# A list scheduler's durations set from a trace, and its priorities changed over 41 trial schedules, in a two-block transformer forward pass

## Chip, core and metric

One core of a Trainium2 chip runs the whole program in one launch. The metric is the device time of one execution in microseconds (us); each figure for a kernel is the median of several executions. TensorE does matmuls (PE in the rows; PEld is its weight load), VectorE is DVE, ScalarE is ACT, GpSimd is POOL, and SyncE (SP) issues most DMAs. Every engine takes its instructions strictly in the order in which they stand in its own stream.

## What is computed

Two transformer layers on 256 tokens of width 1024, batch 1, all in float32. The reference, cut to its frame:

```python
h = rms_norm(x, norm_attn_pre)
parts = split_cols(h @ w_in, IN_SPLITS)
o_a, o_b, o_c, o_d = nsa(...), dilated(...), forgetting(...), mla(...)   # four attentions
merged = sum(sigmoid(h @ w_merge_gate[i]) * (o_i @ w_i) for i in 4 branches)
x = x + rms_norm(merged @ w_o)
x = x + rms_norm(conv_gated_ffn(rms_norm(x)))          # 1024 -> 2 x 2816 -> 1024
# second layer
x = x + mix(retention(...), differential_attention(...)) @ w_out
x = x + cross_attention(rms_norm(x), rms_norm(mem)) @ xo
x = x + (silu(h @ w_gate) * (h @ w_up)) @ w_down       # h = rms_norm(x)
```

The weights, some 150 MB, are read once.

## The kernel before

**Tiling.** Tokens stand as two tiles of 128 (tt = 0, 1). A large matrix product is made of float32r (fp32r) matmuls in three terms: each weight panel of 512 KB (a tile of class `raw`, 128 x 1024) comes in by a DMA on SP, ScalarE casts it to its high part (`hi`), VectorE subtracts to get the low part (`lo = raw - hi`), and `mm3` adds hi x hi, hi x lo and lo x hi in one PSUM bank. These are the rows `bank<-hi,x`, `bank<-lo,x` (weights moving) and `bank<-x,hi`, `bank<-x,lo` (weights stationary). A panel of 1024 columns feeds 12 matmuls of 512 columns. There are 3 `raw`, 8 `hi` and 8 `lo` buffers, so a DMA waits until ScalarE and VectorE have done with a `raw` buffer, and a cast waits until TensorE has done with a `hi` buffer. Activations are transposed on TensorE against `ident` (rows `bank<-ident,k`), and attention works in plain float32 (rows `bank<-k,k`).

**Attention.** `attend` treats two heads: `scores` (four matmuls that stay together, 128x256 and 128x128 twice), then on VectorE a fused add of the bias with a row minimum (in the trace CUSTOM_DVE_ANT_0 and the read of its accumulator), exponentials on ScalarE, a reciprocal and four scalings on VectorE, two times three transposes of the probabilities on TensorE, two copies out of PSUM (one VectorE, one ScalarE), and `values` (four matmuls 64x256 and 64x128). Branch a (nsa) calls it four times.

**The order.** The program is not emitted as it is written. Class `Plan` records every operation with what it reads and writes (6336 operations: 4160 PE, 1084 DVE, 740 ACT, 52 POOL, 300 SP). `Plan.issue` then runs a model of the five engines in time: an operation becomes ready when its predecessors have ended, plus `NEAR` (100 ns) on the same engine or `FAR` (300 ns) on another; an engine that is free takes the ready one with the lowest `prio` that finds its buffers; and the operations are emitted in the order of their modelled starts. `prio` is the number in the program, less 150 for what isn't bulk weight work, less 300 for what is marked urgent; the first DMAs have -4000. `_Op.cost` gives the modelled duration. Buffers are assigned in the same pass. So durations and priorities set the order on each engine, and nothing else does. The helper that emits every operation is the lambda in `add`, so every row of the trace carries its line, L100.

**Places.** The prediction goes to four places: the start (`mats1`: `x` in halves, `gcol`, the panels of `wi0`); branch a's four calls of `attend`, which stand beside the weights of merge gate 1 (`gate(1, "c")`); the first step of the first FFN (`make_ffn`: `natural`, whose evacuation `ev` copies PSUM to `nat`, and `dnstep`, whose panels come from `in_fdn`); and the remaining stretches in which TensorE idles.

Of the kernel before, what the change touches and what calls it, by code (L numbers as in the profile page):

```python
# [19 lines left out]
class Plan:  # L20
# [138 lines left out]
    def issue(self):  # L159
        ops = self.ops  # L160
        succ = [[] for _ in ops]
        left = [len(o.preds) for o in ops]
        ready = [0.0] * len(ops)
        for o in ops:
            for p in o.preds:
                succ[p.n].append(o)
# [3 lines left out]
        order = {}  # L170
        for o in ops:
            o.own = [nm for nm in o.tiles if nm in self.cls]
            for nm in o.own:
                if self.users[nm][0] is o:
                    order.setdefault(self.cls[nm], []).append(nm)
        ptr = {c: 0 for c in order}
        placed = [False] * len(ops)
# [13 lines left out]
        start = [0.0] * len(ops)  # L191
        while done < len(ops):
# [5 lines left out]
            while pend and pend[0][0] <= t:  # L198
                _, n = heapq.heappop(pend)
                heapq.heappush(heaps[ops[n].eng], (ops[n].prio, n))  # L200
            while rel and rel[0][0] <= t:
                u, c, i = heapq.heappop(rel)
                heapq.heappush(free[c], (u, i))
            for e, hp in heaps.items():
# [24 lines left out]
                if e in ("DVE", "ACT") and not o.urgent:  # L229
                    soon = t + self.PATIENCE * o.cost  # L230
                    if any(r <= soon and ops[m].eng == e and ops[m].urgent for r, m in pend):
                        heapq.heappush(hp, (o.prio, n))
                        continue
                for nm in o.own:
# [4 lines left out]
                    self.real[nm] = self.slots[c][place[nm]]  # L239
                    while ptr[c] < len(order[c]) and order[c][ptr[c]] in place:  # L240
                        ptr[c] += 1
                placed[n] = True
                start[n] = t
                if o.dma:
# [3 lines left out]
                    end = dma_free + 900.0  # L248
# [4 lines left out]
                for s in succ[n]:  # L253
# [3 lines left out]
                    ready[s.n] = max(ready[s.n], end + lat)  # L257
# [4 lines left out]
                for nm in o.tiles:  # L262
                    users[nm] -= 1
                    o_end = max(self.last.get(nm, 0.0), end)
                    self.last[nm] = o_end
                    if not users[nm] and nm in self.cls:
                        heapq.heappush(rel, (o_end + self.FAR, self.cls[nm], place[nm]))
                        heapq.heappush(events, o_end + self.FAR)
        self.length = max(tfree.values())
# [3 lines left out]

    reserve = {"k4": 1, "x8": 2, "k2": 3, "x2": 2, "k1": 2, "sm": 4, "PS": 2}

    @property
    def last(self):
        return self.__dict__.setdefault("_last", {})


class _Op:
    def __init__(self, plan, n, eng, go, name, outs, ins, k):
# [8 lines left out]
        elif eng == "PE":  # L291
            n_ = size if name == "matmul" else 128
            passes = 1 if name == "transpose" or ins[0].dtype == F32R else 4
            least = 107.0
            self.cost = max(least, n_ * passes / 2.4)
        elif eng == "ACT":
            extra = sum(isinstance(k.get(x), bass.AP) for x in ("scale", "accum_out"))
            self.cost = 105.0 + 0.8125 * size + 93.0 * extra
        elif eng == "DVE":
# [3 lines left out]
            self.cost = 65.0 + size * (0.52 if two else 1.042) + (45.0 if name == "scalar_tensor_tensor" else 0.0)  # L303
# [4 lines left out]
    def go(self):  # L308
        for part in self.parts:
            part()  # L310
# [1323 lines left out]
```

## Time and profile before

| | us |
|---|---|
| median of 3 runs | 883.85 (882.42 to 883.87) |
| the profiled execution, its own time | 883.68 |
| its span, first to last instruction | 881.9 |
| TensorE busy in the span | 860.0 (98%) |
| TensorE weight load busy | 717.4 (81%) |
| VectorE busy | 639.2 (72%) |
| ScalarE busy | 492.2 (56%) |
| DMA | 156.08 MB, mean 177 GB/s |

The page gives shares of the whole span; a table by stretches of time shows where an engine idles, the list of waits who ended the idle time, and the timeline one engine's instructions in order. Matmuls overlap each other in the rows, since the end of one is modelled: the time that one costs is read from the distance of the starts of two rows, and a busy TensorE can still be slower than it could be.

### The profile page before, as it was taken

To read this page: it belongs to the slowest core of one execution; us is meant where nothing else is said; L and a number is where in the kernel's file an instruction comes from. 1 tells how busy PE (TensorE), PEld (TensorE's weight loads), DVE (VectorE), ACT (ScalarE), POOL (GpSimd) and SP (SyncE) were. 2 spreads that over 40 slices of the span, in tenths; PEclk is the share of its full clock that TensorE was granted. 3 is DMA by queue.
4 is the path that set the end of the run, shared out by engine and by line. 5 is a ranking of instruction groups with operands and counts; after the bars stand their busy time and mean duration, and the time that the engine had idled before them with its cause. 6 is when DMAs were issued, how large, how long until landed. Compare 5 with 4: busy or idle time off the path is not lost.

```text
span 881.9 us, 12156 instructions
## 1 busy us (share of the span) xinstructions
PE 860.0 (98%) x4436; PEld 717.4 (81%) x4436; DVE 639.2 (72%) x1148; ACT 492.2 (56%) x845; POOL 46.3 (5%) x58
## 2 busy tenths in 40 slices
PE   6999998999999999999999999999999999999998
PEld 5789876788887888888877887788888888888886
DVE  6885558867567998887978687967855777666662
ACT  5775454745455676666754457655644565455441
POOL 2100000000001000000010022211100000000000
PEclk9999999999999999999999999999999999999999
DMA  7556743565457577665636654554633577666541
GB/s 244 184 202 196 228 139 96 184 202 192 146 156 245 161 218 216 200 208 171 211 100 212 191 165 147 166 168 156 201 122 96 160 225 229 194 175 198 185 138 49
DMA packets 45185, 156.08 MB, mean 177 GB/s; under 512 B 5262, under 2 KB 6840, under 8 KB 44996
## 3 DMA queue, kind: packets, MB, share of 16 engines
q1 hardware_dynamic: 44228, 153.10, 55.7%
q0 software_dynamic: 896, 2.19, 1.0%
q8 instruction: 35, 0.57, 0.2%
q14 instruction: 26, 0.21, 0.1%
HBM read 154.21 MB, written 1.06 MB: 176 GB/s over the span
## 4 chain that ended last, share of the span: by engine, by line
PE 83%; DVE 7%; DMA 3%; issue 3%; ACT 2%; POOL 1%; SPq 0%; DVEq 0%; POOLq 0%; ACTq 0%
PE bank L100 83%; DVE k L100 4%; DVE lo L100 2%; ACT k L100 2%; DVE x L100 1%; POOL sm L100 1%; DMA raw<-in_fdn 1%; DVE sm L100 1%; DMA raw<-in_wi 1%; DMA sm<-in_ind 1%; DMA sm<-in_dgain 1%; DMA sm<-in_xgain 0%; ACT x L100 0%; ACT hi L100 0%; SPq L100 0%
## 5 line engine op out<-in xcount | busy, mean ns | idle before, releaser
L100 PE MATMUL bank<-hi,x 128*128 128x512 f32 (+3 forms) x1556 | 497.6, 393 | 1.8 <-ACT x L100 1.7
L100 DVE TENSOR_TENSOR lo<-raw,hi 128x1024 fp32r<-128x1024 f32 (+2 forms) x279 | 335.1, 1208 | 102.3 <-ACT hi L100 99.7
L100 ACT CAST hi<-raw 128x1024 fp32r<-128x1024 f32 (+2 forms) x279 | 288.8, 1040 | 139.1 <-PE bank L100 64.3
L100 PEld LDWEIGHTS bank<-hi,x 128*128 128x128 f32 (+1 forms) x1556 | 290.5, 188 | 58.6 <-ACT x L100 2.3
L100 PE MATMUL bank<-lo,x 128*128 128x512 f32 (+3 forms) x786 | 306.5, 391 | 0.4 <-DVE lo L100 0.4
L100 PE MATMUL bank<-x,hi 128*128 128x512 f32 x656 | 228.7, 398 | 0.0
L100 PE MATMUL bank<-x,lo 128*128 128x256 f32 x656 | 171.0, 281 | 0.0
L100 PEld LDWEIGHTS bank<-lo,x 128*128 128x128 f32 (+1 forms) x786 | 147.3, 187 | 27.7 <-DVE lo L100 1.2
L100 PEld LDWEIGHTS bank<-x,hi 128*128 128x128 f32 x656 | 119.3, 188 | 22.8
L100 PEld LDWEIGHTS bank<-x,lo 128*128 128x128 f32 x656 | 124.0, 189 | 7.5
L100 ACT COPY k<-bank 128x256 f32<-128x256 f32 (+5 forms) x116 | 46.0, 399 | 91.1 <-PE bank L100 90.8
L100 PE MATMUL bank<-ident,k 128*128 128x128 f32 (+2 forms) x362 | 59.9, 283 | 12.2 <-DVE k L100 9.2
L100 PEld LDWEIGHTS bank<-ident,k 128*128 128x128 f32 (+2 forms) x362 | 44.5, 142 | 27.5 <-DVE k L100 14.7
L100 POOL TENSOR_TENSOR sm<-sm,nhalf 128x1 f32<-128x1 f32 (+3 forms) x36 | 36.8, 1024 | 511.5 <-DVE sm L100 501.6
L100 DVE TENSOR_TENSOR x<-bank,x 128x512 fp32r<-128x512 f32 (+4 forms) x62 | 36.7, 609 | 28.6 <-PE bank L100 21.2
L100 PE MATMUL bank<-k,k 64*128 64x256 f32 (+12 forms) x364 | 51.2, 332 | 2.7 <-DVE k L100 1.7
L100 PEld LDWEIGHTS bank<-k,k 64*128 64x128 f32 (+4 forms) x364 | 39.9, 180 | 14.0 <-issue 4.7
L100 DVE TENSOR_TENSOR k<-k,bank 128x256 f32<-128x256 f32 (+1 forms) x78 | 32.5, 418 | 23.9 <-ACT k L100 23.4
L100 ACT ACTIVATE k<-bank 128x512 f32<-128x512 f32 (+4 forms) x41 | 19.4, 480 | 44.7 <-PE bank L100 43.1
L100 ACT CAST x<-bank 128x512 fp32r<-128x512 f32 (+2 forms) x49 | 24.5, 515 | 20.7 <-PE bank L100 20.1
L100 DVE SCALAR_TENSOR_TENSOR k<-k,convw,k 128x255 f32<-128x255 f32 x72 | 34.1, 479 | 1.0 <-ACT k L100 0.4
L100 ACT ACTIVATE k<-bank,sm 128x256 f32<-128x256 f32 (+1 forms) x42 | 22.6, 564 | 16.1 <-PE bank L100 9.5
(97 smaller groups left out, 404.9 us busy)
## 6 DMA issues: line engine op xcount, KB each, us to landing
raw<-in_wi SPq DMA_DIRECT2D x42, 512.0 KB, 4.2
raw<-in_up SPq DMA_DIRECT2D x40, 512.0 KB, 4.2
raw<-in_fup SPq DMA_DIRECT2D x36, 512.0 KB, 4.3
raw<-in_wg SPq DMA_DIRECT2D x32, 512.0 KB, 4.1
raw<-in_fdn SPq DMA_DIRECT2D x22, 512.0 KB, 4.4
raw<-in_dn SPq DMA_DIRECT2D x22, 512.0 KB, 4.5
raw<-in_xkv SPq DMA_DIRECT2D x16, 512.0 KB, 4.5
raw<-in_wo SPq DMA_DIRECT2D x8, 512.0 KB, 4.2
```

Source lines behind the costliest of these rows:

```text
L100: op = _Op(self, n, eng, lambda: getattr(target, name)(*map(self.place, a), **{x: self.place(y) for x, y in k.items()}), name, outs, ins, k)
```

## The change

The set of operations, their shapes and their number on each engine stay as they are: 4250 matmul instructions, 300 DMAs on SP and so on in both programs. What changes is the scheduler. `_Op.cost` has other constants: a float32r matmul n/2.4 + 13.5 ns, a transpose 108, other float32 matmuls at four passes + 3; ScalarE 70 or 120 ns + 0.8125 a column and 75 for each operand of one column; VectorE with a term for scalar operands; POOL's power by its columns, not 700 flat. The modelled end of a DMA is 1700 ns after its data instead of 900. The old body of `issue` becomes `trial(prio)`, which also keeps, for each operation, which predecessor was last (`late`) and who freed the buffer that it lacked (`short`). `hurry` walks over the modelled gaps of TensorE, and for each (the first time all of them, then each with chance 0.4) follows up to 14 steps back from the matmul that waited to what ended last, and takes 20, 60 or 150 off the priority of each operation that stood ready for over 50 ns. `issue` runs `trial` once, then 40 times with hurried priorities, and keeps a schedule only if its modelled length is smaller.

```diff
-    def issue(self):
+    def trial(self, prio):
...
-                heapq.heappush(heaps[ops[n].eng], (ops[n].prio, n))
+                heapq.heappush(heaps[ops[n].eng], (prio[n], n))
...
                         if len(free[c]) < need:
                             ok = False
+                            short[n] = c
...
-                    end = dma_free + 900.0
+                    end = dma_free + 1700.0
...
+        return max(tfree.values()), start, place, (ready, late, short)
+
+    def hurry(self, run, prio, share, pick):
+
+        ops = self.ops
+        _, start, _, (ready, late, short) = run
+        new = list(prio)
+        end = 0.0
+        for o in sorted((o for o in ops if o.eng == "PE"), key=lambda o: start[o.n]):
+            gap = start[o.n] - end
+            if gap > 80.0 and pick.random() < share:
+                n, seen = o.n, 0
+                push = pick.choice((20, 60, 150))
+                while n >= 0 and seen < 14 and start[n] > start[o.n] - 25000.0:
+                    by = short.get(n, -1)
+                    if start[n] - ready[n] > 50.0:
+                        new[n] -= push
+                    n = by if by >= 0 and start[n] - ready[n] > 50.0 and start[by] < start[n] else late[n]
+                    seen += 1
+            end = max(end, start[o.n] + o.cost)
+        return new
+
+    def issue(self):
...
+        pick = random.Random(1)
+        prio = [o.prio for o in ops]
+        best = self.trial(prio)
+        for i in range(self.ROUNDS):
+            other = self.hurry(best, prio, 1.0 if i == 0 else 0.4, pick)
+            try:
+                run = self.trial(other)
+            except RuntimeError:
+                continue
+            if run[0] < best[0]:
+                best, prio = run, other
...
+    ROUNDS = 40
...
-            passes = 1 if name == "transpose" or ins[0].dtype == F32R else 4
-            least = 107.0
-            self.cost = max(least, n_ * passes / 2.4)
+            if name == "transpose":
+                self.cost = 108.0
+            elif ins[0].dtype == F32R:
+                self.cost = n_ / 2.4 + 13.5
+            else:
+                self.cost = max(112.0, n_ * 4 / 2.4 + 3.0)
         elif eng == "ACT":
-            extra = sum(isinstance(k.get(x), bass.AP) for x in ("scale", "accum_out"))
-            self.cost = 105.0 + 0.8125 * size + 93.0 * extra
+            extra = sum(isinstance(k.get(x), bass.AP) for x in ("scale", "bias", "accum_out")) + (name == "mul" and len(ins) > 1)
+            self.cost = (70.0 if ps else 120.0) + 0.8125 * size + 75.0 * extra
...
-            self.cost = 65.0 + size * (0.52 if two else 1.042) + (45.0 if name == "scalar_tensor_tensor" else 0.0)
+            aps = len(ins) > 1 and name in ("tensor_scalar", "scalar_tensor_tensor")
+            self.cost = 65.0 + size * (0.52 if two else 1.042) + (60.0 if aps and two else 20.0 if name == "tensor_tensor_reduce" else 0.0)
+        elif name == "tensor_tensor":
+            self.cost = 420.0 + 155.0 * size
```

**The start, SP's stream.** `x_150` is the first token tile and `x_151` the second, each loaded in two halves of 256 KB; `sm_119` is the gain in columns; `raw_63` to `raw_65` are the first three weight panels. Before:

```order
L100 DMA x_150<-in_x 128x512 x2
L100 DMA sm_119<-in_gcol 128x8
L100 DMA raw_63<-in_wi 128x864
L100 DMA raw_64<-in_wi 128x864
L100 DMA raw_65<-in_wi 128x864
L100 DMA x_151<-in_x 128x512 x2
L100 DMA cst<-in_cst 128x832
```

and now:

```order
L101 DMA x_150<-in_x 128x512 x2
L101 DMA x_151<-in_x 128x512
L101 DMA sm_119<-in_gcol 128x8
L101 DMA raw_63<-in_wi 128x864
L101 DMA raw_64<-in_wi 128x864
L101 DMA raw_65<-in_wi 128x864
L101 DMA x_151<-in_x 128x512
L101 DMA cst<-in_cst 128x832
```

One half of the second token tile (its columns 512 to 1023) now stands ahead of the gain and of the three panels. VectorE's square of that half, which needs it, moves with it: from behind the eight low parts of the first transposes to a place ahead of the two scalings of the first token tile that make its transposes possible.

**Branch a's attention, TensorE's stream,** from the second call's transposes of probabilities to its values (`bank<-ident,k` the transposes, `k,k` with 64 columns the values, `hi` and `lo` weights of merge gate 1). Before, two more groups of transposes follow at once:

```order
L100 MATMUL bank_138<-ident,k_101 128x128 x3
L100 MATMUL bank_136<-ident,k_100 128x128 x3
L100 MATMUL bank_137<-k_96,k_117 64x128
L100 MATMUL bank_137<-k_102,k_117 64x128
L100 MATMUL bank_137<-k_96,k_116 64x256
L100 MATMUL bank_137<-k_102,k_116 64x256
L100 MATMUL bank_135<-ident,k_99 128x128 x3
L100 MATMUL bank_138<-ident,k_94 128x128 x3
L100 MATMUL bank_136<-k_84,k_83 128x256
L100 MATMUL bank_141<-k_84,k_83 128x256
```

and now:

```order
L101 MATMUL bank_137<-ident,k_97 128x128 x3
L101 MATMUL bank_141<-ident,k_99 128x128 x3
L101 MATMUL bank_138<-lo_80,x_90 128x512
L101 MATMUL bank_138<-hi_72,x_90 128x512
L101 MATMUL bank_138<-hi_68,x_91 128x512
L101 MATMUL bank_138<-lo_76,x_91 128x512
L101 MATMUL bank_138<-hi_68,x_91 128x512
L101 MATMUL bank_135<-k_96,k_118 64x128
L101 MATMUL bank_135<-k_101,k_118 64x128
L101 MATMUL bank_135<-k_96,k_116 64x256
L101 MATMUL bank_135<-k_101,k_116 64x256
```

Five weight matmuls stand between the transposes and the values that wait for their copies. Counted over the place: before, from the scores of the first call to the last values there stand 26 weight matmuls, 24 transposes, five groups of scores (one of them branch b's) and three of values. Now the first call's scores stand 129 weight matmuls ahead of the next scores, and from those to the last values there are 39 weight matmuls, 22 transposes, four groups of scores and three of values. VectorE's share of the later stretch falls from 20 bias adds, 16 scalings, 4 low parts and 4 copies to 12, 12, 3 and 4.

**The first FFN step, ScalarE's stream** (`hi<-raw` casts of weight panels, `k<-bank` the copy of `ev`; the cast ahead of the copy is that of the first panel of `in_fdn`). Before:

```order
L100 CAST x_90<-bank_135 128x4x128
L100 CAST x_91<-bank_139 128x4x128
L100 CAST hi_70<-raw_65 128x1024
L100 CAST hi_69<-raw_63 128x1024
L100 CAST hi_72<-raw_64 128x1024
L100 COPY k_98<-bank_136 128x256
L100 CAST hi_68<-raw_65 128x1024
```

and now:

```order
L101 CAST x_90<-bank_138 128x4x128
L101 CAST x_91<-bank_137 128x4x128
L101 CAST hi_67<-raw_65 128x1024
L101 CAST hi_69<-raw_63 128x1024
L101 COPY k_100<-bank_142 128x256
L101 CAST hi_68<-raw_64 128x1024
```

The copy out of PSUM, for which the next transposes wait, has changed places with the cast of the `in_fdn` panel.

## Rows read from the trace of the kernel before

**Rows 1.** The page: the span, each engine's busy time (share of the span) and number of instructions.

```profile
span 881.9 us, 12156 instructions
PE 860.0 (98%) x4436; PEld 717.4 (81%) x4436; DVE 639.2 (72%) x1148; ACT 492.2 (56%) x845; POOL 46.3 (5%) x58
```

**Rows 2.** Busy time by stretch of the span (start:end, its length, then busy us and number of instructions on each engine, granted TensorE clock, DMA share, GB/s).

```profile
0.00:20.00 20.00, 11.60 (x48) 9.55 (x49) 12.86 (x39) 11.30 (x26) 4.31 (x11) 1.00 0.73 245
20.00:80.00 60.00, 59.24 (x341) 49.94 (x340) 47.17 (x145) 41.15 (x99) 4.88 (x9) 1.00 0.59 192
124.00:148.00 24.00, 20.64 (x130) 14.38 (x130) 18.75 (x79) 14.11 (x42) 0.00 (x0) 0.93 0.39 121
160.00:175.00 15.00, 14.06 (x82) 10.71 (x82) 13.84 (x44) 9.57 (x21) 1.08 (x2) 1.00 0.54 154
270.00:287.00 17.00, 15.42 (x74) 12.09 (x73) 12.93 (x17) 8.78 (x15) 1.09 (x2) 1.00 0.80 256
455.00:480.00 25.00, 24.43 (x114) 19.32 (x114) 22.06 (x37) 12.67 (x21) 3.08 (x4) 1.00 0.69 217
540.00:580.00 40.00, 38.03 (x218) 30.22 (x217) 36.70 (x99) 27.53 (x67) 7.84 (x8) 1.00 0.43 135
870.00:881.90 11.90, 7.53 (x34) 5.90 (x32) 2.83 (x5) 0.00 (x0) 0.00 (x0) 0.99 0.24 90
```

**Rows 3.** TensorE's waits over the span: tile waited for, total us, times, longest.

```profile
PE bank L100 <- DVE k L100: 10.9, 11, 6.9
PE bank L100 <- ACT k L100: 3.0, 4, 1.1
```

**Rows 4.** TensorE's timeline (start, us, instruction, count, idle before and what ended it) over branch a's calls of `attend`, from the first scores to the last values.

```profile
124.47 0.93 PE L100 MATMUL bank<-k,k 64*128 64x256 f32 x8
125.32 0.50 PE L100 MATMUL bank<-hi,x 128*128 128x512 f32 x1
...
136.97 0.55 PE L100 MATMUL bank<-ident,k 128*128 128x128 f32 x3 [0.75 <-DVE sm L100]
138.78 0.43 PE L100 MATMUL bank<-k,k 128*64 128x128 f32 x2 [1.26 <-DVE k L100]
140.18 0.86 PE L100 MATMUL bank<-k,k 128*64 128x128 f32 x6 [0.97 <-ACT k L100]
...
146.25 0.50 PE L100 MATMUL bank<-k,k 128*64 128x128 f32 x3
```

**Rows 5.** The same table as Rows 2 for that place, and for its end.

```profile
124.50:146.20 21.70, 18.34 (x115) 13.14 (x114) 18.09 (x77) 13.94 (x42) 0.00 (x0) 0.92 0.41 125
140.00:146.00 6.00, 5.82 (x36) 4.21 (x36) 4.43 (x24) 2.09 (x9) 0.00 (x0) 0.72 0.16 60
```

**Rows 6.** VectorE's instructions in that place, by groups (count, busy us, mean ns of one).

```profile
L100 DVE CUSTOM_DVE_ANT_0 k<-bank,big 128x256 f32<-128x256 f32 (+1 forms) x20 | 6.0, 351 | 0.6 <-PE bank L100 0.6
L100 DVE TENSOR_TENSOR lo<-raw,hi 128x1024 fp32r<-128x1024 f32 x4 | 4.9, 1219 | 0.0
L100 DVE TENSOR_SCALAR k<-k,sm 128x128 f32<-128x128 f32 (+1 forms) x16 | 4.1, 316 | 0.0
L100 DVE COPY k<-bank 128x384 f32<-128x384 f32 x4 | 2.2, 553 | 0.2 <-PE bank L100 0.2
```

**Rows 7.** TensorE's timeline where it waits for nothing.

```profile
467.19 0.39 PE L100 MATMUL bank<-lo,x 128*128 128x512 f32 x1
467.42 0.62 PE L100 MATMUL bank<-hi,x 128*128 128x512 f32 x2
467.88 0.60 PE L100 MATMUL bank<-ident,k 128*128 128x128 f32 x4
468.23 0.48 PE L100 MATMUL bank<-lo,x 128*128 128x512 f32 x1
468.54 0.63 PE L100 MATMUL bank<-hi,x 128*128 128x512 f32 x2
```

**Rows 8.** The first FFN step: timelines of ScalarE and of TensorE.

```profile
284.05 1.05 ACT L100 CAST hi<-raw 128x1024 fp32r<-128x1024 f32 x1 [3.82 <-DMA raw<-in_fdn]
285.00 0.36 ACT L100 COPY k<-bank 128x256 f32<-128x256 f32 x1
...
283.96 0.39 PE L100 MATMUL bank<-hi,x 128*128 128x512 f32 x1
285.42 0.66 PE L100 MATMUL bank<-ident,k 128*128 128x128 f32 x4 [1.07 <-ACT k L100]
```

**Rows 9.** The start: timelines of SP, ScalarE, VectorE and TensorE, then one stretch as in Rows 2 and the median time from issue to landing of the halves of `x`.

```profile
1.65 0.42 SPq L100 DMA_DIRECT2D sm<-in_gcol  x1
2.11 1.38 SPq L100 DMA_DIRECT2D raw<-in_wi  x3
...
8.02 1.96 ACT L100 CAST hi<-raw 128x864 fp32r<-128x864 f32 x2 [3.40 <-DMA raw<-in_wi]
...
6.32 0.88 DVE L100 TENSOR_SCALAR k<-x,sm 128x512 f32<-128x512 f32 x2 [0.67 <-POOL sm L100]
...
10.29 0.73 PE L100 MATMUL bank<-hi,x 128*128 128x432 f32 x1 [1.47 <-ACT x L100]
...
3.00:4.00 1.00, 0.00 (x0) 0.00 (x0) 0.00 (x0) 0.11 (x1) 0.00 (x0) 1.00 1.09 284
...
x<-in_x SPq DMA_DIRECT2D x4, 256.0 KB, 5.3
```

More of the change, by code (lines that the diff above doesn't have):

```diff
@@ L2 @@
 import math
+import random
 from contextlib import ExitStack, contextmanager
@@ L157, in glue @@
         self.gluing, self.glued = False, None
-    def issue(self):
+    def trial(self, prio):
         ops = self.ops
-        succ = [[] for _ in ops]
         left = [len(o.preds) for o in ops]
         ready = [0.0] * len(ops)
-        for o in ops:
-            for p in o.preds:
-                succ[p.n].append(o)
+        late = [-1] * len(ops)
         users = {nm: len(u) for nm, u in self.users.items()}
@@ L169, in issue @@
         place = {}
[L170 to L175, printed above, removed]
+        last = {}
+        order = self.order
         ptr = {c: 0 for c in order}
-        placed = [False] * len(ops)
         heaps = {e: [] for e in ("PE", "DVE", "ACT", "POOL", "SP")}
@@ L191, in issue @@
         start = [0.0] * len(ops)
+        freed = {}
+        short = {}
         while done < len(ops):
@@ L252, in issue @@
                 heapq.heappush(events, tfree[e])
-                for s in succ[n]:
+                for s in self.succ[n]:
                     lat = self.NEAR if s.eng == e and not o.dma else self.FAR
@@ L256, in issue @@
                         lat = 0.0
-                    ready[s.n] = max(ready[s.n], end + lat)
+                    if end + lat >= ready[s.n]:
+                        ready[s.n] = end + lat
+                        late[s.n] = n
                     left[s.n] -= 1
@@ L263, in issue @@
                     users[nm] -= 1
-                    o_end = max(self.last.get(nm, 0.0), end)
-                    self.last[nm] = o_end
+                    o_end = max(last.get(nm, (0.0, 0)), (end, n))
+                    last[nm] = o_end
                     if not users[nm] and nm in self.cls:
-                        heapq.heappush(rel, (o_end + self.FAR, self.cls[nm], place[nm]))
-                        heapq.heappush(events, o_end + self.FAR)
-        self.length = max(tfree.values())
+                        heapq.heappush(rel, (o_end[0] + self.FAR, self.cls[nm], place[nm], o_end[1]))
+                        heapq.heappush(events, o_end[0] + self.FAR)
@@ new lines, in issue @@
+    def issue(self):
+        ops = self.ops
+        self.succ = [[] for _ in ops]
+        for o in ops:
+            for p in o.preds:
+                self.succ[p.n].append(o)
+        self.order = {}
+        for o in ops:
+            o.own = [nm for nm in o.tiles if nm in self.cls]
+            for nm in o.own:
+                if self.users[nm][0] is o:
+                    self.order.setdefault(self.cls[nm], []).append(nm)
+        pick = random.Random(1)
[9 more added lines that the diff above has]
+                best, prio = run, other
+        self.length, start, place, _ = best
+        self.real = {nm: self.slots[self.cls[nm]][i] for nm, i in place.items()}
```

12 lines of the change are left out of this document (5 added, 7 removed).

## Prediction

> **What bounds the kernel now.** First the page's busy times: TensorE is busy for 860.0 of 881.9 us [rows 1], so every other engine counts only where TensorE waits for it. Then the table by stretches, to see where the 21.9 us of TensorE's idle time lie: 20.00 - 11.60 = 8.4 at the start and 11.90 - 7.53 = 4.4 at the end, where the first data come and the last go, and between them 0.8 (20 to 80), 3.4 (124 to 148), 0.9 (160 to 175), 1.6 (270 to 287), 0.6 (455 to 480) and 2.0 (540 to 580) [rows 2], 9.2 in all. The list of waits says whom it waits for: VectorE 10.9 us with the 6.9 of the start, ScalarE 3.0 [rows 3]. In the three largest of these stretches VectorE is the busiest engine beside it (18.75 of 24, 12.93 of 17, 36.70 of 40 us).
>
> Idle time isn't all of the loss. At the place with most of it the starts are 146.25 - 124.47 = 21.8 us apart [rows 4]. What stands there costs much less where nothing is waited for: three 512-column weight matmuls from 467.19 to 467.88, 0.23 us each; four transposes and the matmul behind them 0.66, so 0.108 a transpose [rows 7]; a group of four scores 0.85, from 124.47 to 125.32 [rows 4], and I take as much for one of values. 26 x 0.228 + 24 x 0.108 + 8 x 0.85 = 15.3 us. So 6.5 us are lost there, of which the table shows 21.7 - 18.34 = 3.4 as idle. Part of the rest is the clock: from 140 to 146 the granted clock is 0.72, a mean between 1.2 and 2.4 GHz, after TensorE stood still for 0.97 us and 1.26 us shortly before [rows 4, 5]; 6.0 x 0.28 = 1.7 us. The remainder are waits under the modelled ends of matmuls.
>
> By busy time alone the place could give 3.4 us. The Trainium skill, Perfetto Trace Analysis, Identifying the Most-Contended Engine, says that matmul busy time doesn't measure the headroom because matmuls are pipelined, and to look at weight loads instead. The trace bears that out here (15.3 us of work in 21.8, and weight loads busy 81% against 98%); by busy time the sum below would be some 3 us smaller, 879.6.
>
> **The change, part by part.** No operation is added or removed, so all is in the order; the work of TensorE stays the same. The durations in the plan cost the chip nothing.
>
> *Start.* Half of the second token tile now leaves SP ahead of the gain and of the three weight panels. In the trace the first weight matmul at 10.29 waits for ScalarE, whose casts begin when a panel lands at 8.02 [rows 9], and in the hundreds of instructions behind it TensorE has only 0.8 us of idle to absorb a delay [rows 2]. One issue costs 2.11 - 1.65 = 0.46 us; the transfer costs 262,144 bytes / 284 GB/s = 0.92 [rows 9]. If the transfers overlap, only the issue counts. I take the transfer, +0.9; bounds +0.5 and +2.3 (the upper one is the rival of the other sign, below).
>
> The Trainium skill, DMA: Bandwidth & Descriptors, Queues, rings and completion order, speaks against this move: one issuing engine's descriptors are consumed in ring order on each DMA engine, so the panels would stand behind all of the half. No run here shows it apart from the landings; with the rule the term is 0.9, without it 0.5.
>
> *Branch a's attention.* Before, VectorE is the bound: it is busy for 18.1 of 21.7 us [rows 5], against 15.3 us of TensorE's work, because four calls of `attend` and four low parts of weights fall together. Now the first call is 129 weight matmuls (29 us) ahead, and from the second call's scores to the last values TensorE has 39 x 0.228 + 22 x 0.108 + 7 x 0.85 = 17.2 us of work. VectorE's large groups were 6.0 + 4.9 + 4.1 + 2.2 = 17.2 us [rows 6]; with 12 of 20, 3 of 4, 12 of 16 and 4 of 4 of them left they are 3.6 + 3.7 + 3.1 + 2.2 = 12.6, and with the small ones in the same ratio 13.3. So TensorE has more to do than VectorE, where it had less, and the values that waited 1.26 us for a copy have five weight matmuls, 1.14 us, ahead of them. The clock's 1.7 us go too if TensorE no longer stands. What is late next is the chain inside one call. I leave 1.0 us for it: -5.5, bounds -6.5 (all of it) and -2.0 (branch b's softmax and the low parts, which stood behind, now press in the same way some 10 us later).
>
> *First FFN step.* TensorE's distance 283.96 to 285.42 is 1.46 us against 0.23 for the matmul: 1.2 lost. The transposes wait for ScalarE's copy at 285.00, which has stood behind a cast that waited 3.82 us for its panel until 284.05 [rows 8]. Now the copy stands ahead of that cast; the accumulator that it reads is ready when the last matmul ends, so it runs in the 3.82 us. Its cover is that wait; if the panel came early, nothing would be lost before either. What the cast feeds, matmuls over 10 us later, hides the 0.36 us by which it moves. -1.2, bounds -1.2 and 0.
>
> *The other stretches* (20 to 80, 160 to 175, 455 to 480, 540 to 580) have 0.8 + 0.9 + 0.6 + 2.0 = 4.3 us of idle. The order changes in all of them in the same manner: low parts and casts move against softmax work, a few matmuls at a time. I take two thirds of the idle, -2.8; bounds 0 and -8, the latter with what lies under it in the ratio of the first place (6.5 / 3.4).
>
> *New waits.* A stream in which hundreds of instructions are moved will wait in new places, where the plan's durations are off by a few hundred ns. From the trace of before none can be named with a time; the nearest rows are its waits, up to 1.26 us each [rows 4]. I take one such, +1.3; bounds 0 and +4 (three).
>
> Sum: 0.9 - 5.5 - 1.2 - 2.8 + 1.3 = -7.3 us. Against the profiled execution's own 883.68 that is 876.4; the median of the runs is 0.17 higher, so 876.5.
>
> **Rivals.**
>
> *More comes.* All of branch a's 6.5, the first FFN step's 1.2, twice the idle of the other stretches, 8, and the start at 0.5: -15.2, 868.6. For it: the hidden part was as large as the idle where it could be worked out. Against: those stretches have VectorE at 79 to 92% of the time, so there is little room to move it. Anything from 866 to 872.
>
> *VectorE's work is only moved.* The rest of branch a's softmax, branch b's and the low parts of gate 1 follow each other from 148 to 175 now, where VectorE is at 13.84 of 15 us already [rows 2]; if they press there, branch a gives 2.0, the others nothing, and the start and new waits take 2.2: with the first FFN step's 1.2, -1.0, and up to 4 us of gain. 880 to 885, half of it within 0.2% of no change.
>
> *The modelled gain isn't on the chip.* The modelled length chose the order, and the chip has its own. Then the sum is 0 up to the new waits, 882 to 885.5.
>
> *Slower: VectorE's square at the start.* The square of the half that is moved stands in VectorE's stream ahead of the two scalings at 6.32 [rows 9], from which all first transposes come. If that half lands in time, it costs some 0.1 us. The halves' median from issue to landing is 5.3 us [rows 9]: issued at 1.65 it lands at 7.0, and with the square's 0.7 the scalings begin at 7.7, 1.3 us late; with the panels' 0.9 that is up to 2.3 us. It decides if the half lands after 5.6 and the other terms come to nothing: 886.0. Against: the casts on ScalarE hide most of the 1.3, as the first weight matmul waits for them.
>
> **How the numbers follow.** The forecast, 872 to 880, has 0.58; more than that 0.14; a gain below it, 880 to 882, 0.10; within 0.2% (1.8 us: 882.1 to 885.6), which is about what a measurement of this kernel can tell from no change, 0.10; slower 0.08. So faster 0.82, same 0.10, slower 0.08. The range 869.5 to 884.0 leaves out half of the first rival (0.07), half of what lies within 0.2% (0.05) and the slower case (0.08), 2 in 10; the bounds of the terms go further, but they rarely fall together.
>
> **What would show it.** In the changed kernel's table by stretches, 20 us or more around branch a's attention with TensorE idle for under 1 us and a granted clock of 1.00 there, and no second place with over 2 us idle: right. The transposes of the first FFN step's `ev` with no wait for ScalarE, although a cast behind them waits for `in_fdn`: right. The first weight matmul at 11.0 to 11.3 instead of 10.29: right on the start; at 10.3 the transfers overlapped, at over 12 the square held it. The prediction is wrong if TensorE's busy time grows where its idle falls, with starts no closer (the loss only hides), or if a wait for VectorE of over 2 us stands between 148 and 180.

## The result, and the profile after

| | before | changed |
|---|---|---|
| median, us (6 runs each) | 883.40 (881.89 to 884.33) | 879.12 (878.52 to 879.54) |
| ratio, 95% interval | | 0.9947 (0.9937 to 0.9957) |
| span of the profiled execution | 881.9 | 877.0 |
| TensorE busy | 860.0 | 858.2 |

The change makes the kernel faster by 4.3 us, 0.5%. The forecast was -7.3 us, so its sign and its case (872 to 880) hold, and its size is 3 us too large.

Of the 4.9 us of span, 1.8 are less busy time of TensorE and 3.1 less idle time. The table by stretches of the changed kernel (columns as in [rows 2]) shows where it idles now:

```profile
0.00:20.00 20.00, 11.44 (x42) 9.30 (x43) 12.16 (x37) 10.82 (x24) 3.58 (x11) 1.00 0.78 237
20.00:80.00 60.00, 59.10 (x335) 48.84 (x334) 46.23 (x147) 40.96 (x99) 5.52 (x9) 1.00 0.58 184
...
124.00:148.00 24.00, 23.52 (x137) 17.48 (x137) 17.62 (x61) 13.34 (x36) 0.00 (x0) 1.00 0.45 139
...
270.00:287.00 17.00, 15.40 (x75) 12.21 (x74) 12.08 (x20) 9.76 (x15) 0.46 (x1) 1.00 0.74 244
...
540.00:580.00 40.00, 38.34 (x219) 31.15 (x216) 38.52 (x102) 27.32 (x65) 7.06 (x8) 1.00 0.46 135
```

From 124 to 148 only 0.5 us are idle, against 3.4 before. The stretch with the first FFN step idles as long as before (1.6 us), and so nearly does 540 to 580 (1.7 against 2.0). TensorE's waits over the span (as [rows 3]):

```profile
PE bank L101 <- DVE k L101: 10.5, 9, 7.1
PE bank L101 <- ACT k L101: 1.3, 1, 1.3
```

**A finer way to compare.** Both traces hold the same matmuls, so the start of the same matmul can be looked up in both. At many moments both programs have done the same operations on all engines; between two such moments, the difference of the distances is what that stretch gained or lost. This table is worked out so for the changed kernel and for every experiment, in us against the profiled execution of before. The stretches are named by before's time. The names are told below; with e2, e7 and e11 four to eight matmuls stand on the other side of some borders. Each row is of one execution, mostly within 0.5 us of the kernel's median, but e1's is its fastest (2.0 us under the median), e7's its slowest (2.2 over) and e6's 0.9 over.

```
                                   7-18  18-38  38-71 71-213 213-279 279-286 286-323 323-518 518-877   sum
changed kernel                    +1.17  -0.58  +1.13  -5.67   -0.11   -1.27   +1.65   -1.61   +0.03  -5.25
e1 new durations, no loop         +0.57  -0.22  -0.48  -1.97   -0.13   -1.27   +0.43   -1.65   +1.15  -3.57
e2 old durations, loop            -1.27  +0.38  +0.04  -4.98   -1.06   -0.81   +0.21   -0.38   -1.68  -9.55
e5 change, seed 2                 +0.25  -0.22  -0.50  -1.83   -0.11   -1.27   +1.19   -1.61   +0.49  -3.62
e6 old durations, loop, seed 2    +1.22  +0.55  +0.77  -3.89   +0.02   +0.29   +0.05   +0.19   -1.38  -2.19
e7 change, old TensorE durations  +1.37  -1.67  +0.61  -6.89   +0.23   -0.83   +0.38   -0.60   +3.21  -4.18
e3 branch a only                  +0.22  -0.63  +0.06  -6.15   +0.01   +0.27   -0.00   +0.68   -0.08  -5.62
e4 best of both                   +0.34  -0.64  +0.04  -6.12   -0.13   +1.01   +0.04   -1.61   -0.57  -7.64
e8 two repairs                    +1.79  -0.41  +1.13  -6.17   -0.11   -1.27   +0.06   -1.58   -0.03  -6.59
e9 start evacuations              -0.87  +0.15  +1.12  -6.13   -0.12   -1.26   +0.11   -1.37   -0.20  -8.57
e10 no low parts                  +0.34  -0.61  +0.01  -1.33   +0.02   +0.04   +0.05   +0.06   -0.11  -1.54
e12 first call ahead              +0.17  -0.62  +0.01  -0.51   -0.00   +0.09   +0.05   +0.16   +0.00  -0.65
e11 joined                        -0.64  -0.15  -0.56  -6.84   +0.19   -0.82   -0.16   -1.28   -1.56 -11.83
```

In the changed kernel the place of branch a gives 5.7 us and the stretch from 323 to 518 another 1.6. The first FFN step gives 1.3 and loses 1.65 right behind; the first 71 us lose 1.7. The mechanism can be seen by the rows of each place. Branch a, TensorE's timeline (as [rows 4]), and 6 us of that place in the table by stretches:

```profile
133.29 1.72 PE L101 MATMUL bank<-k,k 64*128 64x256 f32 x16
134.94 0.50 PE L101 MATMUL bank<-hi,x 128*128 128x512 f32 x1
...
139.82 0.82 PE L101 MATMUL bank<-ident,k 128*128 128x128 f32 x6
140.39 0.48 PE L101 MATMUL bank<-lo,x 128*128 128x512 f32 x1
...
142.02 0.87 PE L101 MATMUL bank<-k,k 128*64 128x128 f32 x8 [0.22 <-DVE k L101]
143.15 0.88 PE L101 MATMUL bank<-ident,k 128*128 128x128 f32 x6 [0.26 <-DVE k L101]
...
140.00:146.00 6.00, 5.52 (x38) 4.20 (x37) 4.37 (x15) 2.69 (x11) 0.00 (x0) 1.00 0.33 95
```

Between the scores, transposes and values there are now weight matmuls (`bank<-hi,x`, `bank<-lo,x`). The waits of 0.75, 1.26 and 0.97 us are gone, the largest here is 0.26, and the granted clock stays at 1.00 (before, 0.72 in these 6 us).

The first FFN step, timelines of ScalarE and TensorE (as [rows 8]):

```profile
279.41 0.37 ACT L101 COPY k<-bank 128x256 f32<-128x256 f32 x1 [0.90 <-PE bank L101]
281.34 1.05 ACT L101 CAST hi<-raw 128x1024 fp32r<-128x1024 f32 x1 [1.56 <-DMA raw<-in_fdn]
282.29 1.93 ACT L101 ACTIVATE k<-bank,convw 128x256 f32<-128x256 f32 x4
284.10 0.38 ACT L101 COPY k<-bank 128x256 f32<-128x256 f32 x1
...
280.12 0.61 PE L101 MATMUL bank<-ident,k 128*128 128x128 f32 x4
...
284.53 0.44 PE L101 MATMUL bank<-ident,k 128*128 128x128 f32 x2 [1.26 <-ACT k L101]
```

As predicted, the copy at 279.41 stands ahead of the cast, and its four transposes wait for nothing. But the cast of the second `in_fdn` panel waits 1.56 us for its DMA at the head of ScalarE's stream, and behind it stand the convolution and the copy of the next step. The wait has moved by one step. It is the wait of the same cast: before, too, the cast that the copy stood behind was that of the second `in_fdn` panel, not of the first, as the section on the change has it. Of the chain that ended last before, its panel, issued at 276.65, lands at 283.97, and the cast begins at 284.05:

```profile
276.65 7.32 DMA raw<-in_fdn
```

The start, timelines of ScalarE, VectorE and TensorE (as [rows 9]):

```profile
7.68 0.91 ACT L101 CAST hi<-raw 128x864 fp32r<-128x864 f32 x1 [3.29 <-DMA raw<-in_wi]
...
10.10 0.91 ACT L101 CAST hi<-raw 128x864 fp32r<-128x864 f32 x1
...
11.86 1.40 ACT L101 ACTIVATE x<-bank,sm 128x128 fp32r<-128x128 f32 x5 [0.42 <-DVE x L101]
...
11.47 0.35 DVE L101 SCALAR_TENSOR_TENSOR x<-bank,sm,x 128x128 fp32r<-128x128 f32 x1 [0.44 <-ACT x L101]
...
10.00 0.73 PE L101 MATMUL bank<-hi,x 128*128 128x432 f32 x1 [0.96 <-ACT x L101]
...
13.10 1.09 PE L101 MATMUL bank<-hi,x 128*128 128x432 f32 x2 [0.52 <-DVE x L101]
```

The first weight matmul isn't late (10.00 against 10.29), nor is the first panel (7.68 against 8.02). New is a wait at 13.10: ScalarE and VectorE write the first transposes out of PSUM in turns and wait for each other.

The first matmuls are also slow in both kernels, which the table doesn't show. TensorE's timeline before, and in the changed kernel:

```profile
13.42 0.56 PE L100 MATMUL bank<-lo,x 128*128 128x432 f32 x1
14.50 0.45 PE L100 MATMUL bank<-lo,x 128*128 128x432 f32 x1
15.18 0.36 PE L100 MATMUL bank<-lo,x 128*128 128x432 f32 x1
15.75 0.36 PE L100 MATMUL bank<-lo,x 128*128 128x432 f32 x1
...
16.15 0.56 PE L101 MATMUL bank<-lo,x 128*128 128x432 f32 x1
17.23 0.46 PE L101 MATMUL bank<-lo,x 128*128 128x432 f32 x1
19.39 0.36 PE L101 MATMUL bank<-lo,x 128*128 128x432 f32 x1
19.96 0.35 PE L101 MATMUL bank<-lo,x 128*128 128x432 f32 x1
```

From 13.42 to 14.50 there are three matmuls of 432 columns, 0.36 us each, which is 432 / 1.2 GHz; from 15.18 to 15.75 three take 0.19 us each (432 / 2.4 GHz is 0.18). So TensorE runs at the lower of its two clock levels until 14.5 us before and until 17.2 in the changed kernel. The record of the granted clock in these traces begins only then (14.68 and 17.44 us), and the table counts what isn't recorded as 1.00.

### The profile page after: what moved, and what is told of

The parts are those of the page before. It is cut to its first block, busy times and chain, and to the rows that moved or that the text cites. A ratio compares the mean times of both kernels' runs of the same rounds, so it can differ in the third digit from the quotient of the medians.

```text
span 877.0 us, 12151 instructions
## 1 busy us (share of the span) xinstructions
PE 858.2 (98%) x4436; PEld 715.8 (82%) x4436; DVE 639.8 (73%) x1148; ACT 490.9 (56%) x845; POOL 47.3 (5%) x58
## 4 chain that ended last, share of the span: by engine, by line
PE 82%; DVE 7%; ACT 4%; issue 2%; DMA 2%; POOL 1%; SPq 0%; DVEq 0%; POOLq 0%; ACTq 0%
PE bank L101 82%; DVE k L101 3%; ACT k L101 2%; DVE lo L101 2%; ACT hi L101 1%; DVE x L101 1%; POOL sm L101 1%; DMA raw<-in_fdn 1%; DVE sm L101 1%; DMA raw<-in_xkv 1%; DMA raw<-in_wi 1%; ACT junk L101 0%; ACT L101 0%; SPq L101 0%; ACT x L101 0%
## 5 line engine op out<-in xcount | busy, mean ns | idle before, releaser
L101 PEld LDWEIGHTS bank<-ident,k 128*128 128x128 f32 (+2 forms) x362 | 44.2, 140 | 25.1 <-DVE k L101 15.6
L101 PE MATMUL bank<-k,k 64*128 64x256 f32 (+12 forms) x364 | 49.0, 325 | 0.7 <-DVE k L101 0.7
L101 PEld LDWEIGHTS bank<-k,k 64*128 64x128 f32 (+4 forms) x364 | 37.7, 176 | 10.8 <-issue 4.1
L101 ACT CAST x<-bank 128x512 fp32r<-128x512 f32 (+2 forms) x49 | 24.4, 515 | 17.9 <-PE bank L101 17.2
```

The lines of the kernel that those rows point to most:

```text
L101: op = _Op(self, n, eng, lambda: getattr(target, name)(*map(self.place, a), **{x: self.place(y) for x, y in k.items()}), name, outs, ins, k)
```

## The experiments

e1 to e4, e5 to e8 and e9 to e11 each ran together on one chip with runs of the kernel before, e12 by itself with such runs; a ratio is to the before beside it.

**e1: the new durations without the loop.**

```diff
-    ROUNDS = 40
+    ROUNDS = 0
```

> The new durations with a single schedule (no loop). Theory, that the loop brings about half of what branch a's attention gains and itself causes the loss in the first 20 us: the stretch from 71 to 211 us gains some 2.5 us instead of 5.7, the start is as before, and the time is 880 to 882. Rival, that the durations do it all and the loop only polishes a modelled length: 879, as with the loop. Rival, that the loop does it all: 883.

Measured 881.86 us, ratio 0.9977 (0.9967 to 0.9987). The durations alone give 1.8 us, the loop the other 2.7. From 71 to 213 us the durations give 2.0 and the loop 3.7 more, two thirds of it; the loss of the first 71 us (+1.7) comes from the loop, as without it they gain 0.1. The theory holds, with a reserve: the row of e1 is of its fastest execution, so most executions gain less than it shows, and where they lose isn't on record.

**e2: the durations of before with the loop.** `_Op.cost` and the 900 ns behind a DMA as before, `trial`, `hurry` and 40 rounds as changed.

```diff
-                    end = dma_free + 1700.0
+                    end = dma_free + 900.0
...
-            if name == "transpose":
-                self.cost = 108.0
...
+            passes = 1 if name == "transpose" or ins[0].dtype == F32R else 4
+            least = 107.0
+            self.cost = max(least, n_ * passes / 2.4)
```

> The durations of before (900 ns behind a DMA's data too) with the loop of 40 rounds. Theory, that the loop finds part of branch a's gain whatever the durations, since it acts on what stands late in that place: 3 to 5 us there, little elsewhere, 879 to 881. Rival, that a loop over wrong durations only moves the modelled length: 883, or slower by new waits.

Measured 873.61 us, ratio 0.9882 (0.9870 to 0.9895): faster than the whole change by 5.5 us, which neither theory had. It gains nearly as much in branch a, and besides at the start, at 213 to 279 and behind 518. This raised the question that e5 to e7 answer.

**e5, e6, e7: is it the durations or the random numbers?** e5 is the whole change with `random.Random(2)`, e6 is e2 with `random.Random(2)`, e7 the whole change with TensorE's durations of before.

```diff
-        pick = random.Random(1)
+        pick = random.Random(2)
```

> The whole change with other random numbers in the loop (seed 2 for 1). Theory, that the new durations hold the loop back whatever the numbers: 878 to 882, within 2 us of the changed kernel's 879.1. Rival, that the 5.5 us between it and the loop over the old durations (873.6) are luck of one sequence: about as likely 874 as 880.

> The durations of before with the loop and seed 2. Theory (the old durations are the better ground for the loop): 872 to 876 again. Rival (luck): anything from 873 to 881.

> The whole change, but TensorE's durations as before: 213 ns a 512-column matmul, where the trace shows 0.228 us, so TensorE is planned some 6% too fast. Theory, that this error is what leaves slack in front of TensorE on the chip (whoever feeds it is planned to be early): 873 to 876, as with all the old durations. Rival, that another constant (1700 ns for 900 behind a DMA, ScalarE's or VectorE's) makes the difference: 878 to 881.

| loop over | seed 1 | seed 2 |
|---|---|---|
| the new durations | 879.12, 0.9947 (0.9937 to 0.9957) | 880.10, 0.9960 (0.9943 to 0.9977) |
| the old durations | 873.61, 0.9882 (0.9870 to 0.9895) | 880.17, 0.9965 (0.9953 to 0.9977) |
| new, TensorE's old | 877.26, 0.9935 (0.9921 to 0.9950) | |

The theory that the old durations are the better ground falls with e6: with other numbers they give 880.2, no better than the new ones. e7 lies between; its +3.21 behind 518 is of the profiled execution, in which the granted clock is 0.50 from 546.6 to 553.4 us, after waits of 1.34 and 1.04 us. Two sequences over the same durations differ by up to 6.6 us, more than the whole change brings, so the 5.5 us of e2 are taken as the luck of one sequence. Two seeds on each side are few; a difference of a few us between the durations isn't excluded.

**e3 and e4: do places add?** In these and in all that follow, `issue` doesn't plan. It emits the operations in an order from a list (joined from the schedules of the kernels above) and gives out the buffers in turn:

```diff
-        best = self.trial(prio)
...
+        for n in order:
+            for nm in ops[n].own:
+                if nm not in self.real:
+                    self.real[nm] = free[self.cls[nm]].pop(0)
+            ops[n].go()
```

> The order of before, except for the stretch from 71 to 211 us, which has the changed order. Theory, that a place's time depends on the order in that place alone (both programs have done the same operations on every engine at these two moments): 883.4 - 5.7 = 877.7, which is less than the changed kernel's 879.1, since the loss ahead of 71 us isn't taken. Rival, that a gain at one place is given back by waits behind it: 879 to 883.

> Each stretch with the order that had the shorter time there: before up to 71 us, changed from 71 to 277, before to 322, changed to 593, before to 645, changed from there. Theory (gains of places add): -5.7 - 0.1 - 1.6 - 0.2 - 0.2 = -7.8, 875.6, faster than both. Rival (given back behind): 877 to 879.

e3: 877.37 us, ratio 0.9928 (0.9914 to 0.9941). e4: 876.09 us, ratio 0.9913 (0.9895 to 0.9931). Both are within 0.5 us of the sum of their places, so a place's time is set by the order in it, and what is gained there isn't waited off later. Branch a's place alone is worth more than the whole change by the medians (the two intervals overlap a little), as the table has it too (-5.7 of -5.25). The list has its own small effect: where its order is that of before, the first 38 us still differ by -0.3 to -0.45 us (e3, e4, e10, e12), and joints (where two orders meet) cost up to 1.0 (e4 at 279). Differences of half a microsecond in one stretch are not read below.

**e8: two repairs of the changed order.** The third panel's cast and low part move behind the evacuations (the copies of transposes out of PSUM) at the start; the DMA of `in_norm_mix` moves behind the second panel of `in_fdn`.

```diff
-L101 DMA g<-in_norm_mix
 L101 DMA raw<-in_fdn
+L101 DMA g<-in_norm_mix
```

> The changed kernel's order with two local edits, read by stretches. Start: the third panel's cast (ScalarE) and low part (VectorE) stand behind the evacuations of the first transposes, as before; SP's order stays as changed. Theory, that these two held the evacuations and not the half of x that SP issues early: the wait of 0.9 us at 12.0 goes and the first 37 matmul instructions take 1.0 us less. Rival (SP's move): no change there. First FFN step: the 512 KB of the gain in_norm_mix are issued behind the second panel of in_fdn, not ahead of it. Theory, that the new wait of 1.26 us at 283 is that panel's late landing: it lands some 1.8 us earlier, and the stretch loses 1.2 us. Rival (the transfers overlap): the panel lands as late, no change. Both right: 876.9; one: 878; none: 879.1.

Measured 876.81 us, ratio 0.9925 (0.9911 to 0.9940). The FFN half is right: 286 to 323 falls from +1.65 to +0.06. ScalarE's timeline there:

```profile
275.86 1.05 ACT L171 CAST hi<-raw 128x1024 fp32r<-128x1024 f32 x1 [2.16 <-DMA raw<-in_fdn]
279.45 0.37 ACT L171 COPY k<-bank 128x256 f32<-128x256 f32 x1 [2.54 <-PE bank L171]
279.72 1.05 ACT L171 CAST hi<-raw 128x1024 fp32r<-128x1024 f32 x1
280.67 1.94 ACT L171 ACTIVATE k<-bank,convw 128x256 f32<-128x256 f32 x4
```

The second panel has landed when its cast comes (279.72, no wait), and the convolution behind it begins at 280.67 instead of 282.29. The start half is wrong: 7 to 18 us loses 1.79, no less than before the repair. That the time is still that of both right (876.9) is luck: 0.5 us of it come from 71 to 213, where the order is the changed kernel's. ScalarE and VectorE still hand over to each other with waits of 0.42 to 0.86 us, now without the cast between. That gave the next theory.

**e9: the evacuations.** As e8, but ScalarE's eight evacuations stand ahead of VectorE's eight; SP's order and the early square stay as changed.

> The kernel of the two repairs with another start: SP's order and VectorE's early square of the half of x stay as changed, but ScalarE's eight evacuations of the first transposes stand together ahead of VectorE's eight, as before, instead of alternating with them. Theory, that the start is lost by the alternation (in the changed kernel and in that with two repairs ScalarE and VectorE wait for each other there, 0.42 to 0.86 us a time): the first 37 matmul instructions take as long as before, 1.2 to 1.8 us less than with the repairs, and the time is 875.2. Rival (the early half of x and its square, as predicted): they still take 0.5 to 1 us more than before, 876 to 876.8.

Measured 875.57 us, ratio 0.9909 (0.9895 to 0.9924). From 7 to 38 us it is 0.7 better than before, where e8 is 1.4 worse; timelines of ScalarE, VectorE and TensorE:

```profile
9.58 2.17 ACT L171 ACTIVATE x<-bank,sm 128x128 fp32r<-128x128 f32 x8
...
10.75 2.16 DVE L171 SCALAR_TENSOR_TENSOR x<-bank,sm,x 128x128 fp32r<-128x128 f32 x8
...
12.04 0.56 PE L171 MATMUL bank<-lo,x 128*128 128x432 f32 x1
12.40 0.92 PE L171 MATMUL bank<-hi,x 128*128 128x432 f32 x2
```

Eight in 2.17 us and no wait, with the half of `x` still issued early. So the alternation cost the start its time and not SP's move. The four kernels that alternate (the changed one, e6, e7, e8) lose 1.2 to 1.8 us from 7 to 18, e6 and e7 without the half of `x` ahead; the other nine lie between -1.3 and +0.6. Part of the difference is the clock at the start: the matmuls stand 0.36 us apart until 15.6 us in e8 and until 13.8 in e9. Not all of that is the order's, as the moment differs by 1 us between kernels with the same order there (14.5 before, 15.4 to 15.7 in e3, e4, e10 and e12).

**e10: is VectorE's work the bound of branch a's place?** Before's order from a list, with four operations of VectorE left out:

```diff
-            ops[n].go()
+            if n not in (1152, 1155, 1158, 1161):
+                ops[n].go()
```

> The order of before throughout, but the four low parts of merge gate 1's panels that VectorE takes off in branch a's place (129.5 to 138.2 us, 1.22 us each) are left out, so that the matmuls there read what the buffers held before. They aren't part of an attention call's chain. Theory, that VectorE's amount of work binds this place: it gets 3 to 4.9 us shorter with no matmul moved, 879 to 880.5. Rival, that the order of TensorE's own stream or the chain inside a call binds it: under 1 us, 882.5 to 883.5.

Measured 881.54 us, ratio 0.9979 (0.9967 to 0.9991); the place gives 1.3 us, nearer to the rival's 1 than to the 3 to 4.9 of the theory. VectorE is now busy for 14.9 of 21.7 us, against 18.1 [rows 5], and the place still lasts 21.8 - 1.3 = 20.5 us, with 15.3 us of work for TensorE. The clock falls as before (0.92 over the place). What holds it stands, behind the place's row of the table, in the timelines of ScalarE and TensorE:

```profile
124.50:146.20 21.70, 19.62 (x125) 13.70 (x123) 14.86 (x75) 13.85 (x42) 0.00 (x0) 0.92 0.36 122
...
137.42 0.51 ACT L169 ACTIVATE k<-k,sm 128x256 f32<-128x256 f32 x1 [0.56 <-DVE sm L169]
137.83 0.19 ACT L169 ACTIVATION_READ_ACCUMULATOR k<-k,sm 128x1 f32 x1
137.92 0.46 ACT L169 COPY k<-bank 128x384 f32<-128x384 f32 x1
...
136.25 0.43 PE L169 MATMUL bank<-k,k 128*64 128x128 f32 x2
138.43 1.54 PE L169 MATMUL bank<-k,k 128*64 128x128 f32 x6 [1.75 <-ACT k L169]
```

TensorE's values wait for ScalarE's copy, which stands behind an exponential of the next call, which waits for VectorE's row minimum. The chain goes through both engines, and no weight matmul stands in TensorE's order meanwhile.

**e12: the first call ahead, alone.** Before's order from a list, with only the front of the first call where the changed kernel has it.

> The order of before, with one thing of the changed order alone: the front of branch a's first attention call (its four scores, its row minima, exponentials, scalings and the first two transposes, 18 operations) stands some 120 matmul instructions earlier, at 100 us, among weight matmuls, where the changed kernel has it. The other three calls and the four low parts stay pressed together. Theory, that the place lost time because four chains ran with too few weight matmuls beside them, so that each chain taken out of it gives its share: 1.4 to 3 us less, 880.5 to 882. Rival, that the order of the remaining three calls and of the work behind them must change too: under 0.6 us, 883 to 883.5.

Measured 882.89 us, ratio 0.9989 (0.9978 to 0.9999); the stretch gives 0.5 us. The rival holds: the three waits stay, TensorE's timeline:

```profile
135.84 0.55 PE L169 MATMUL bank<-ident,k 128*128 128x128 f32 x3 [0.73 <-DVE sm L169]
137.65 0.43 PE L169 MATMUL bank<-k,k 128*64 128x128 f32 x2 [1.27 <-DVE k L169]
139.05 1.54 PE L169 MATMUL bank<-k,k 128*64 128x128 f32 x6 [0.97 <-ACT k L169]
```

**e11: joined.** An order from a list, joined of five schedules by the stretches in which each was shortest.

> An order joined from the schedules that were shortest by stretches: at the start the first weight panel is issued ahead of the gain's columns, then the new durations without the loop up to 74 us, the run with TensorE's old durations from there to 270, the loop over the old durations to 408, the changed kernel to 523, the loop over the old durations to 606, then the changed kernel. By the stretches' own times: -2.0 - 6.9 - 1.6 - 1.6 - 1.7 - 0.2 = -14.0 us against before, 869.5. Theory, that places add: 868.5 to 871. Rival, that joints between schedules that were never planned together cost new waits: 872 to 876.

Measured 871.63 us, ratio 0.9861 (0.9848 to 0.9873): faster than both kernels, by 11.9 and 7.5 us, and than e2 (873.61). By the stretches it is 2.2 us short of the sum, 0.7 of it up to 71 us and 0.8 in the first FFN step (213 to 323); so joints cost something, as the rival has it, but most adds; the time lies between the ranges of the two. TensorE's waits and two stretches of the table:

```profile
PE bank L172 <- DVE k L172: 7.9, 4, 6.7
PE bank L172 <- DVE sm L172: 0.7, 1, 0.7
...
124.00:148.00 24.00, 24.00 (x152) 17.44 (x151) 20.37 (x83) 15.21 (x46) 0.00 (x0) 1.00 0.33 105
...
540.00:580.00 40.00, 40.00 (x215) 33.37 (x214) 36.84 (x72) 26.37 (x50) 8.81 (x9) 1.00 0.59 184
```

Of the 7.9 us, 6.7 are the first data. In branch a's place VectorE is busier here (20.37 of 24 us) than before (18.75, [rows 2]), and TensorE has no idle time there.

## Why the prediction was right in sign and too large

**What bounds the kernel.** Right: TensorE bounds it, and the gain came from its idle time (3.1 us) and from slow stretches under busy rows (1.8). That the idle time understates the loss was right in branch a's place: its idle fell by 2.9 us (124 to 148) and its time by 5.7. That 879.6, by busy time alone, would have been close to the result is luck: errors cancel in it.

**Start, predicted +0.9.** Measured +0.6 (7 to 38 us), within the bounds, but by another mechanism. The step "half of the second token tile now leaves SP ahead" failed as a cause: by its own sign, a first weight matmul at 10.3 meant overlapped transfers, and it came at 10.00. The first panel's cast begins at 7.7, 8.4 and 7.8 us in the three kernels with the half ahead, and at 7.1 to 8.0 in the seven with the same order otherwise. That is +0.4 on the mean, about the price of one issue (the lower bound), but the seven differ by 0.9 among themselves, so neither the issue nor the transfer is shown. The Trainium skill, DMA: Bandwidth & Descriptors, Queues, rings and completion order, says that each DMA engine consumes descriptors in ring order, by which the prediction put the panels behind all of the half, +0.9; the landings here neither show nor exclude that. What cost the time was the alternation of ScalarE and VectorE (e9), which no term had, since the order on those two engines at the start was not part of it. No term had the clock of the start either, at its lower level until 17.2 us instead of 14.5.

**Branch a's attention, predicted -5.5.** Measured -5.7, and with the rest as before -6.2 (e3). Both are of 71 to 213 us, which also holds the stretch from 160 to 175 that the prediction counted with the others (-0.6 of its -2.8): the orders differ throughout, and the two can't be told apart. The signs came: under 1 us of idle time, clock 1.00. The reason given was half right. "VectorE is the bound" was worth 1.3 us when its work was taken away (e10), and "the first call is 129 weight matmuls ahead" 0.5 by itself (e12). Neither is the mechanism alone. What carries it is the third thing that the prediction named: weight matmuls ahead of each step that waits. Before, between 133.8 and 145.6 us no weight matmul stands in TensorE's order (58 rows of attention in a row), so each hand-over of the chain through VectorE and ScalarE is a wait, and the clock falls; in the changed order some stand between nearly every two steps. No single run here took that alone away, so it is what e10 and e12 leave over, and the rows of e11 (VectorE busier, TensorE without idle) agree. So do the orders taken together, in part: the three that keep 58 such rows in a row (before, e10, e12) gain 0 to 1.3 us from 71 to 213, the others, with at most 16 to 40, gain 1.8 to 6.9. But that length alone doesn't rank them (e1 and e5 have 24 and gain 2.0 and 1.8, e2 has 40 and gains 5.0). Of the 5.7 us, the clock is 1.7: 0.92 over 21.7 us before [rows 5], 1.00 after. In e10 and e12 it is 0.92 over the place as before, so what they gain is without it.

**First FFN step, predicted -1.2.** Measured -1.27 where it was said. The step that failed is "what the cast feeds ... hides the 0.36 us": what counted was not what the cast feeds but what is queued behind it. The second panel's cast, the one that the copy had been moved ahead of, waited at the head of ScalarE's stream with the next step's convolution and copy behind it: +1.65. The load of `in_norm_mix` (512 KB) goes out between the two panels; moved behind them, the loss is gone (e8).

**The other stretches, predicted -2.8.** Measured -1.6 from 323 to 518 (0.9 of it behind 480, where TensorE had shown no idle time), 0.0 behind 518 and -0.1 from 213 to 279; from 38 to 71, which was counted here, +1.1; 160 to 175 is in branch a's figure. The step "I take two thirds of the idle" failed at 540 to 580, where 1.7 of 2.0 us stayed.

**New waits, predicted +1.3 (one).** There were two losses, 1.1 (38 to 71, where one wait of 0.73 at 50.20 shows) and 1.65 (at 283): +2.8, within the bounds of 0 to +4. With these the terms are +0.6 - 5.7 - 1.3 - 1.7 + 2.8 = -5.3; the first matmul starts 0.2 later (7.08 against 6.86), which leaves 5.1 against the 4.9 of the span. So of the 2.4 us by which the prediction was too large in span, the new waits are 1.5 and the other stretches 1.1.

**The rivals.** More comes: not in this kernel, though e11, at 871.6, shows that orders with as much exist. VectorE's work only moved: no, from 148 to 180 the longest wait for it is 0.5 us. The slower case: the moved half did land after 5.6 (its square starts at 5.92), but the scalings were only 0.22 us late (6.54 against 6.32) and the casts hid it, as the text against it said. The modelled gain not on the chip: no, 4.3 us came. How well the modelled length ranks orders is not shown, as no run gives it; schedules that were all kept for a smaller one gave anything from 873.6 to 880.2.

## What to carry to other kernels

Compare two orders of one program by the starts of the same matmuls at moments when both have done the same work: places add to within some 2 us of 12, so the best order of each place can be kept and joined, and that was worth nearly three times the change itself. A search on a modelled length is a lottery of a few us; run several of its results and let the chip choose. Where a chain of steps passes through several engines, look for independent matmuls between its steps in TensorE's order: the place here that gained most had none for 12 us. Before an instruction that waits for a DMA, ask what is queued behind it on its engine, for as many steps as the wait is long.

## Not expected of the hardware

- The same 512 KB panel, the first of `in_fdn`, landed anywhere from 4.9 to 8.8 us after its issue. It took 4.9 to 5.2 (before, e3, e6, e10, e12) with `in_norm_mix` (512 KB) issued 2.2 us behind it on the same queue and a load of 512 KB by GpSimd 0.7 us behind; 7.8 and 8.8 (changed, e4) with these 1.8 and 0.3 us behind; 6.2 and 5.3 (e8, e9) with GpSimd's 0.3 us behind and `in_norm_mix` behind both panels. Which of the two slows it is not shown.
- A load of 4 KB can cost more than its issue: with the gain's columns (128x8) ahead of the first panel, and no half of `x` more, the panel's cast begins at 7.1 to 8.0 us (seven kernels); with them behind it, at 6.4 to 6.6 (e2, e6, e7, e11). The issue is 0.46 us of that.
- A granted clock of 1.00 in the table can mean that none is on record: at the start the 432-column matmuls stand 0.36 us apart, the lower level, until 14.5 us before, 17.2 in the changed kernel (with its wait at 13.10) and 13.8 in e9 (without it), and 0.20 behind.
